# Padding between the pools of a hybrid attention and RWKV block, so that both operands of each 512-column product start at the same byte address modulo 512

## The chip, the core and the metric

The kernel runs on one core of one Trainium2 chip. The metric is the device time of one execution in microseconds (us). The engines are TensorE (PE; its weight loads are shown apart, as PEld), VectorE (DVE), ScalarE (ACT), GpSimd (POOL) and SyncE (SP, which only issues transfers here). They run independently, each with its own queue of instructions in program order, and meet at semaphores.

## The reference

One layer on x of 2048 rows and 1024 columns, in float32:

```python
h   = rms_norm(x, pre_mix_g);  proj = h @ w_in          # 1024 -> 5376 columns
y_a = chunk_band_attention(q, k, v, rel_bias)           # 8 heads, chunks of 64, 8 chunks back
y_b = rwkv7_time_mix(p_rwkv, ...)                       # 8 heads, a recurrence over time
merged = gate_a * (y_a @ proj_a) + gate_b * (y_b @ proj_b)
x = x + rms_norm(merged @ w_out, post_mix_g)
u = square(relu(rms_norm(x, pre_ffn_g) @ w_up)) @ w_down  # 1024 -> 4096 -> 1024
x = x + rms_norm(u, post_ffn_g)
```

## The kernel before

**Products in three terms.** Large products are not done in plain float32. Each operand is split into a rounded high part and a rest, both of the type float32r, and `mm3` (L73) adds three products: high times high, high times rest, rest times high. Each is one matmul with a stationary operand of 128x128 and a moving operand of 128x512, into one bank of PSUM. The split takes one cast on ACT (L70) and one subtraction on DVE (L71).

**Stages.** The 2048 rows are four groups of 512. For each group come: the RWKV part (`phase_rwkv`: dense products `psd` of `dense`, L89, then chunked linear algebra in plain float32, an inverse on DVE and the recurrence), the attention (`phase_attention`; it also computes the second branch product, `ps_p` of `branch`, with the RWKV output), and the merge (`phase_merge`: the first branch product, `ps_p`, then the output projection `ps_o`, L1028; the next group's norm runs beside it, in groups 0 to 2). After the four groups the feed-forward part runs in two halves, each an up stage (`phase_up`, `ps_u`) and a down stage (`phase_down`, `ps_dn`, L1290), both with one level of Strassen's scheme: seven products in place of eight.

**Where operands lie.** On-chip memory (SBUF) is given out in pools. A pool takes a stretch of each partition beside the pool that was opened before it, and gives each of its tiles a place there; pools that are marked "right" are stacked from the other end. A pool that closes leaves its place to the next. So the size of one tile shifts the start of all that lies behind it. Nothing in the kernel before chooses these starts; they follow from the sizes.

From the allocation of the two programs, the start of the moving and of the stationary operand of each 512-column float32r product, modulo 512 bytes:

| product | count | moving, stationary before | after |
|---|---|---|---|
| dense `psd` | 4032 | 320, 320 | 480, 480 |
| second branch `ps_p` (attention) | 384 | 320, 320 | 480, 480 |
| first branch `ps_p` (merge) | 384 | 480, 320 | 480, 480 |
| output projection `ps_o`, groups 0 to 2 | 576 | 320, 192 | 480, 480 |
| output projection `ps_o`, group 3 | 192 | 320, 320 | 480, 480 |
| up `ps_u` | 2688 | 320, 480 | 480, 480 |
| down `ps_dn` | 2688 | half 320, 320, half 480, 480 | 480, 480 |
| low-rank `ps_z`, `ps_a` (L327, L328) | 64 | 288, 320 | 320, 320 |
| gate `ps_g` (L661) | 48 | 288, 288 | 320, 320 |
| attention scores `ps_s` of 512 columns | 16 | 320, 320 | 480, 480 |

**What sets the order.** A scheduling layer (Tile) places each engine's instructions and adds the waits; a tile's place is free again when its last reader is done. So a tile that moves to other addresses can change what its first writer waits for. n2 (L391) is a small tile of the RWKV part: POOL fills it with ones (L392) and copies the reciprocal squared norms into it (L396), POOL and DVE read it (L399, L462, L487). n2t (L387) is what it is copied from. T (L506) is the workspace of the inverse, X (L505, L507) the inverse itself, which starts as a copy of the identity. The carry copies (L298, L299) hand the last column of one group to the next.

Of the kernel before, what the change touches and what calls it, by code (L numbers as in the profile page):

```python
# [9 lines left out]
F32 = mybir.dt.float32  # L10
# [8 lines left out]
P = 128  # L19
# [6 lines left out]
GT = G // P  # L26
C = 64
NC = G // C
# [14 lines left out]
def advance(steps, n=None):  # L43

    while n is None or n > 0:
        if next(steps, steps) is steps:
            return
        n = n and n - 1


class Block:
# [70 lines left out]
    def constants(self, ctx, mixing):  # L122
        tc, nc, a = self.tc, self.nc, self.a
        keep = ctx.enter_context(tc.tile_pool(name="const", bufs=1))
# [5 lines left out]
        nc.vector.memset(self.nhalf, -0.5)  # L130
        self.ssq = keep.tile([P, self.NG, GT, 2], F32, name="ssqo")
        self.g2c = keep.tile([P, KB], F32, name="g2c")
        self.bones = cp.tile([P, P], F32, name="bones")
        nc.vector.memset(self.bones, 0.0)
        for h in range(2):
# [208 lines left out]
    def rwkv_pre(self, g, p, rp, NA, between=lambda: None):  # L344
# [39 lines left out]
        pss = self.pa.tile([P, GT, 2], F32, tag="a", name="ps_ss")  # L384
        for t in range(GT):
            nc.tensor.matmul(pss[:, t], sq[:, t * P : (t + 1) * P], self.bones2, start=True, stop=True)
        n2t = self.tp.tile([P, GT, 2], F32, tag="n2t", bufs=2, name="n2t")  # L387
        nc.vector.tensor_scalar(n2t, pss, 1e-24, None, ALU.max)
        nc.vector.reciprocal(n2t, n2t)

        n2 = rp.tile([P, NC, 2], F32, tag="n2", name="n2")  # L391
        nc.gpsimd.memset(n2, 1.0)  # L392
        n2v = n2.rearrange("p (t h) e -> p h t e", h=2)
        for par in range(2):
# [103 lines left out]
    def rwkv_inverse(self, NA, rp):  # L498

        nc, ip = self.nc, self.ip  # L500
        N = ip.tile([P, 32, 32], F32, tag="N", name="N")
        nc.vector.transpose(
            N, NA.rearrange("p q c t -> p t (q c)")[:, 0:32, None, :].to_broadcast((P, 32, 2, 2 * NC))
        )
        X = ip.tile([P, 32, 16], F32, tag="X", name="X")  # L505
        T = ip.tile([P, 144], F32, tag="T", name="T")  # L506
        nc.scalar.copy(X, self.x0)  # L507
        for s in range(31):
            n, m = 31 - s, s // 2 + 1
            t = T[:, 0 : n * m].rearrange("p (a b) -> p a b", b=m)  # L510
            nc.vector.tensor_tensor(
                t,
                N[:, s + 1 : 32, s, None].to_broadcast((P, n, m)),
                X[:, s : s + 1, 0:m].to_broadcast((P, n, m)),
                ALU.mult,
            )
            nc.vector.tensor_tensor(X[:, s + 1 : 32, 0:m], X[:, s + 1 : 32, 0:m], t, ALU.add)
            yield
        X1 = ip.tile([P, 2, NC, 32], F32, tag="X1", name="X1")
        nc.vector.transpose(X1.rearrange("p q c (j d) -> p j d (q c)", d=2), X.rearrange("p r j -> p j r"))  # L520
        XD = ip.tile([P, 2, NC, 32], F32, tag="N", name="XD")
        nc.vector.transpose(XD, X1)
        XT = rp.tile([P, 2, NC, C], F32, tag="XT", bufs=1, name="XT")
        for par in range(2):
            r0 = par * C
            nc.gpsimd.memset(XT[r0 + 32 : r0 + 64, :, :, 0:32], 0.0)
            nc.scalar.copy(XT[r0 + 32 : r0 + 64, :, :, 32:64], XD[r0 + 32 : r0 + 64])
        for par in range(2):
            nc.scalar.copy(XT[par * C : par * C + 32, :, :, 0:32], XD[par * C : par * C + 32])
        self.X1, self.XT = X1, XT  # L530
# [406 lines left out]
    def phase_attention(self, g):  # L937
        tc, nc = self.tc, self.nc
        self.yctx = ExitStack()
        yp = self.yctx.enter_context(tc.tile_pool(name="ya", bufs=1, side="right", reuse_waits="tile"))  # L940
        self.ya = self.alloc_y(yp)
        self.bp = self.yctx.enter_context(tc.tile_pool(name="br", bufs=2, side="right", reuse_waits="tile"))
        with ExitStack() as ctx:
            e = ctx.enter_context
            self.ap = e(tc.tile_pool(name="at", bufs=2, reuse_waits="tile"))
            pp = e(tc.tile_pool(name="atp", bufs=1, reuse_waits="tile"))
            self.psc = e(tc.tile_pool(name="atps", bufs=1, space=PSUM, reuse_waits="tile"))
            self.pt = e(tc.tile_pool(name="atpt", bufs=1, space=PSUM, reuse_waits="tile"))
            self.pv = e(tc.tile_pool(name="atpv", bufs=2, space=PSUM, reuse_waits="tile"))
            self.pts, self.npt = [], 0  # L950
            for i in range(2):
                t = [pp.tile([P, 6, 2 * P], F32R, name=f"PT{x}{i}") for x in "hl"]
                for y in t:
                    nc.gpsimd.memset(y[:, 0, P : 2 * P].bitcast(F32), 0.0)
                    nc.gpsimd.memset(y[:, 5, 0:P].bitcast(F32), 0.0)
                self.pts.append(t)

            self.place = pp.tile([2 * GT, GT, P], F32, name="place")
            nc.gpsimd.memset(self.place, 1.0)
            pl = self.place.rearrange("e q (h d) -> e q h d", d=C)  # L960
            nc.gpsimd.affine_select(
                pl, pl, [[-1, GT], [-GT, 2], [0, C]], ALU.is_equal, 0.0, base=0, channel_multiplier=1
            )
            self.unscaled = {}
            beside = iter(())
            if g:
                beside = self.residual(
                    g - 1, pp, lambda: self.pd.tile([P, 4, P], F32, tag="d", name="ps_ht")
                )
            for p in range(NP):  # L970
                self.att_pair(g, p, beside)
            y = self.load_y()
            self.finish(NP - 1)
            for i in range(KB):
                nc.gpsimd.dma_start(self.md[i], self.branch(y, 1, i))
# [147 lines left out]
    def phase_up(self, half, zp, rp, cb, pn, early):  # L1123
# [6 lines left out]
        with ExitStack() as ctx:  # L1130
# [7 lines left out]
            X = zp.tile([P, 7, G], F32, tag="z", name="X")  # L1138
            T = {
                n: [tb.tile([P, KH, G], F32R, name=n + x) for x in "hl"] for n in ("t4", "b22", "t2", "t3", "t1")  # L1140
            }

            def operands():
                td, g1 = self.td[half], self.ht[2 * half + 1]
                for n, src in (
                    ("t2", td[:, 3]), ("t3", td[:, 1]), ("t1", td[:, 0]), ("b22", g1[:, hi4]), ("t4", td[:, 2])
                ):
                    h, l = T[n]
                    for k in (0, 2):
# [5 lines left out]
            def product(l, r, pool, tag):  # L1155
                ps = pool.tile([P, G], F32, tag=tag, name="ps_u")
                self.mm3(ps, [(l[0][:, k], l[1][:, k], r[0][:, k], r[1][:, k]) for k in range(KH)])
                return ps
# [11 lines left out]
            def hidden(dst, src, x):  # L1170

                nc.vector.tensor_tensor(dst, src, x, ALU.add)  # L1172
                nc.scalar.activation(dst, dst, AF.Relu)
                nc.scalar.activation(dst, dst, AF.Square)  # L1174
# [10 lines left out]
            def sums(i, x):  # L1185
                for o, l, r, op in ((3, X[:, 2], X[:, 1], ALU.add), (4, X[:, 3], x, ALU.subtract),
                                    (5, x, X[:, 2], ALU.subtract), (6, X[:, 0], X[:, 4], ALU.subtract)):
                    nc.vector.tensor_tensor(X[:, o], l, r, op)  # L1188
                    keep(o, i, X[:, o])
# [10 lines left out]
            for i in range(FF // P // 2):  # L1200
# [25 lines left out]
                w = up.tile([P, G], F32, tag="w", name="w")  # L1226
                nc.vector.tensor_tensor(q, p1, product(S2, T["t2"], pn, "dn"), ALU.add)
                if last is not None:
                    sums(*last)
                nc.vector.tensor_tensor(w, q, product(S3, T["t3"], pn, "dn"), ALU.add)  # L1230
                ps = product(S1, T["t1"], pn, "dn")
                hidden(X[:, 1], w, ps)
# [128 lines left out]
    def run(self):  # L1361
        tc, e = self.tc, None
        with ExitStack() as ctx, ExitStack() as mixing:
# [11 lines left out]
            for g in range(self.NG):  # L1375
                self.phase_rwkv(g, sums)
                self.phase_attention(g)
                with ExitStack() as c:
                    cmb = c.enter_context(tc.tile_pool(name="p1", bufs=1, reuse_waits="tile"))
                    sp = c.enter_context(tc.tile_pool(name="p0", bufs=2, reuse_waits="tile"))  # L1380
                    pt = c.enter_context(tc.tile_pool(name="p0p", bufs=2, space=PSUM, reuse_waits="tile"))
                    op = c.enter_context(tc.tile_pool(name="mo", bufs=1, reuse_waits="tile"))
                    b = cmb.tile([P, 4, G], F32, tag="cmb", name="cmb")
                    o = [op.tile([P, D], F32, name=f"o{t}") for t in range(GT)]
                    beside = next(sums)([b[:, i] for i in range(4)])
                    advance(beside, 1)
                    self.phase_merge(g, o, op, self.phase_norm(g + 1, sp, pt) if g + 1 < self.NG else iter(()), beside)
                    for t in range(GT):
                        self.nc.gpsimd.dma_start(self.od[g][t], o[t])
# [4 lines left out]
            rp = e(tc.tile_pool(name="raw", bufs=4, side="right", reuse_waits="tile"))  # L1394
# [58 lines left out]
```

## Time and profile before

| what | value |
|---|---|
| median of 3 runs | 3409.09 us (3408.39 to 3412.6) |
| profiled execution | 3405.34 us, with a span of 3403.6 us |
| mean granted TensorE clock | 0.984 |
| PE, PEld busy | 96%, 77% |
| DVE, ACT, POOL busy | 66%, 46%, 17% |
| DMA | 592.57 MB, mean 174 GB/s |

The span is the time from the first to the last instruction of the profiled execution. A row of the timeline gives start, duration, engine, line, operation, output and inputs, and how many equal instructions follow each other. In a row of windows the number behind "x" counts the instructions that lie in the stretch or reach over its edges. A matmul's own duration overlaps the next one's; how fast products run is read from the distance between their starts.

### The profile page before, as it was taken

Reading aid. Unit: us, or ns where it says so; the run is one execution under the profiler, and the core shown is the slowest. Engines: PE = TensorE matmul, PEld = TensorE weight load, DVE = VectorE, ACT = ScalarE, POOL = GpSimd, SP = SyncE. Lnnn points to the kernel's source line nnn. Section 1 sums busy time; section 2 is a strip of 40 time slices with the busy share of each in tenths; the row PEclk is TensorE's granted clock in tenths of the full one; section 3 lists DMA queues with packets and bytes.
Section 4 is the critical chain, followed back from the end, with each engine's and each line's share of the span. In section 5 each row is a group of like instructions: output and inputs, shape, how many; then the busy total and the mean of one; then the engine's idle time right before and its main releaser. Section 6 shows DMA issues by size and latency. Waiting matters only on the chain. (4 is left out here: it accounts for less than half of the span.)

```text
span 3403.6 us, 50503 instructions
## 1 busy us (share of the span) xinstructions
PE 3260.4 (96%) x18993; PEld 2623.8 (77%) x18993; DVE 2232.1 (66%) x3703; ACT 1576.3 (46%) x2575; POOL 593.5 (17%) x1101
## 2 busy tenths in 40 slices
PE   7999999999999999999999999999999999999998
PEld 5777777777877777877777787778788877787887
DVE  5775666775675775665766765777655657774465
ACT  4434634444644434654344654544543444454343
POOL 2122012122111222111221110122211111210000
PEclk9999999999999999999999999999999999999999
DMA  5235374246464236555325547654777875446565
GB/s 148 88 114 186 109 229 127 66 152 225 156 225 131 84 112 213 192 178 170 99 76 190 197 127 236 228 182 152 248 262 240 284 229 186 164 152 223 191 209 181
DMA packets 448669, 592.57 MB, mean 174 GB/s; under 512 B 26324, under 2 KB 313248, under 8 KB 448424
## 3 DMA queue, kind: packets, MB, share of 16 engines
q1 hardware_dynamic: 390184, 408.94, 38.6%
q0 software_dynamic: 49024, 163.61, 13.1%
q10 hardware_dynamic: 9216, 16.78, 1.4%
q8 instruction: 149, 2.44, 0.3%
q14 instruction: 96, 0.79, 0.1%
HBM read 425.37 MB, written 167.01 MB: 174 GB/s over the span
## 5 line engine op out<-in xcount | busy, mean ns | idle before, releaser
L1290 PE MATMUL ps_dn<-fop 128*128 128x512 f32 x2688 | 620.0, 393 | 8.4 <-ACT fop L70 5.8
L1290 PEld LDWEIGHTS ps_dn<-fop 128*128 128x128 f32 x2688 | 507.4, 189 | 119.0 <-ACT fop L70 6.6
L79 PE MATMUL psd<-hh,whi 128*128 128x512 f32 x1344 | 543.7, 405 | 12.2 <-ACT whi L70 8.2
L79 PE MATMUL psd<-hl,whi 128*128 128x512 f32 x1344 | 541.0, 402 | 0.0
L79 PE MATMUL psd<-hh,wlo 128*128 128x512 f32 x1344 | 538.5, 401 | 1.3 <-DVE wlo L71 1.3
L70 ACT CAST whi<-wraw 128x1024 fp32r<-128x1024 f32 (+1 forms) x296 | 255.6, 864 | 587.8 <-PE psd L79 383.9
L71 DVE TENSOR_TENSOR wlo<-wraw,whi 128x1024 fp32r<-128x1024 f32 (+1 forms) x296 | 293.1, 991 | 225.4 <-ACT whi L70 208.4
L79 PEld LDWEIGHTS psd<-hh,whi 128*128 128x128 f32 x1344 | 257.0, 191 | 65.0 <-ACT whi L70 8.9
L79 PEld LDWEIGHTS psd<-hh,wlo 128*128 128x128 f32 x1344 | 256.5, 191 | 51.3 <-DVE wlo L71 2.7
L79 PEld LDWEIGHTS psd<-hl,whi 128*128 128x128 f32 x1344 | 256.9, 191 | 49.8 <-issue 0.2
L71 DVE TENSOR_TENSOR fop<-xraw,fop 128x1024 fp32r<-128x1024 f32 x112 | 137.0, 1224 | 185.0 <-ACT fop L70 184.2
L70 ACT CAST fop<-xraw 128x1024 fp32r<-128x1024 f32 x112 | 117.5, 1049 | 265.9 <-PE ps_dn L1290 213.9
L1177 POOL DMA_DIRECT2D xd<-X x192 | 104.1, 542 | 406.2 <-ACT X L1174 351.8
L71 DVE TENSOR_TENSOR fop<-wdraw,fop 128x1024 fp32r<-128x1024 f32 x112 | 136.6, 1219 | 20.6 <-ACT fop L70 20.3
L70 ACT CAST fop<-wdraw 128x1024 fp32r<-128x1024 f32 x112 | 117.4, 1048 | 32.0 <-DMA wdraw<-in_w_down_dram 25.7
L857 DVE CUSTOM_DVE_ANT_0 sc<-bias,ps_s 128x640 f32<-128x640 f32 (+4 forms) x128 | 93.8, 733 | 57.7 <-PE ps_pt L868 31.9
L79 PE MATMUL ps_p<-yh,whi 128*128 128x512 f32 x256 | 105.1, 412 | 16.5 <-ACT whi L70 14.0
L872 ACT CAST PTh<-ps_pt 128x640 fp32r<-128x640 f32 (+4 forms) x128 | 80.0, 625 | 79.2 <-PE ps_pt L868 78.4
L70 ACT CAST s12h<-s 128x1024 fp32r<-128x1024 f32 x32 | 33.6, 1052 | 174.2 <-PE ps_u L79 174.2
L873 DVE TENSOR_TENSOR PTl<-ps_pt,PTh 128x640 fp32r<-128x640 f32 (+4 forms) x128 | 94.3, 737 | 29.6 <-ACT PTh L872 29.2
L862 ACT ACTIVATE sc<-sc,mn 128x640 f32<-128x640 f32 (+4 forms) x128 | 97.6, 763 | 19.2 <-DVE mn L857 18.4
L79 PE MATMUL ps_p<-yh,wlo 128*128 128x512 f32 x256 | 105.6, 413 | 0.6 <-DVE wlo L71 0.5
(368 smaller groups left out, 6879.2 us busy)
## 6 DMA issues: line engine op xcount, KB each, us to landing
wraw<-in_w_in_dram SPq DMA_DIRECT2D x168, 512.0 KB
xraw<-xd SPq DMA_DIRECT2D x112, 512.0 KB
xd<-X POOLq DMA_DIRECT2D x192, 256.0 KB, 5.1
wraw<-in_w_up_dram SPq DMA_DIRECT2D x80, 512.0 KB
wdraw<-wd SPq DMA_DIRECT2D x64, 512.0 KB
wdraw<-in_w_down_dram SPq DMA_DIRECT2D x48, 512.0 KB
gd<-gate ACTq DMA_DIRECT2D x64, 256.0 KB
cmb<-in_w_down_dram POOLq DMA_DIRECT2D x64, 256.0 KB, 4.7
```

What stands on the lines that cost most here:

```text
L70: self.nc.scalar.copy(hi, src)
L71: self.nc.vector.tensor_tensor(lo, src, hi.bitcast(F32), ALU.subtract)
L79: mm = nc.tensor.matmul(ps, l, r, start=n == 0, stop=n == last).ins
L857: nc.vector.tensor_tensor_reduce(sc[:, 0:n], bias[:, s0:640], pss[:, c0 : c0 + n], 1.0, 3.0e38, ALU.add, ALU.min, mn,)
L862: nc.scalar.activation(sc[:, 0:n], sc[:, 0:n], AF.Exp, scale=-1.0, bias=mn, accum_out=sm[:, col : col + 1])
L872: nc.scalar.copy(hv, pst[:, 0:nk])
L873: nc.vector.tensor_tensor(lv, pst[:, 0:nk], hv.bitcast(F32), ALU.subtract)
L1177: nc.gpsimd.dma_start(self.xd[q][i // 2][:, i % 2], src)
L1290: nc.tensor.matmul(ps, o[:, l, k, sl], o[:, r, k], start=start and n == 0, stop=stop and n == end)
```

## The change

Three tiles are added that nothing reads or writes: 160 bytes in the pool of constants, 320 bytes in the attention's pool (after the four head pairs, ahead of the tiles that hold the RWKV output), and 128 bytes in the norm's pool beside the merge, in groups 0 to 2. Two tiles get smaller: T has 136 numbers in place of 144, n2t one buffer in place of two. n2 leaves the RWKV pool of three buffers and goes to the pool of temporaries with two.

```diff
         self.g2c = keep.tile([P, KB], F32, name="g2c")
+        keep.tile([P, 40], F32, name="pad")
...
-        n2t = self.tp.tile([P, GT, 2], F32, tag="n2t", bufs=2, name="n2t")
+        n2t = self.tp.tile([P, GT, 2], F32, tag="n2t", bufs=1, name="n2t")
...
-        n2 = rp.tile([P, NC, 2], F32, tag="n2", name="n2")
+        n2 = self.tp.tile([P, NC, 2], F32, tag="n2", bufs=2, name="n2")
...
-        T = ip.tile([P, 144], F32, tag="T", name="T")
+        T = ip.tile([P, 136], F32, tag="T", name="T")
...
                 self.att_pair(g, p, beside)
+            self.ap.tile([P, 80], F32, tag="pad", bufs=1, name="pad")
             y = self.load_y()
...
                     sp = c.enter_context(tc.tile_pool(name="p0", bufs=2, reuse_waits="tile"))
+                    if g + 1 < self.NG:
+                        sp.tile([P, 32], F32, tag="pad", bufs=1, name="pad")
```

The order of instructions on PE and on SP is the same in both programs. On POOL and ACT a few move. On POOL, around the end of the second pair of group 1 (n2_5772 and n2_5775 are that pair's n2), before:

```order
L396 COPY n2_5772<-n2t_5769 64x4 x4
L399 TENSOR_TENSOR mN_5778<-mI_86,n2_5772 128x512 x2
L436 DMA bvd1_466<-r_5629 128x512
L299 COPY carry_96<-pr_6013 128x1
L298 COPY pr_6121<-carry_96 128x1
```

and now:

```order
L397 COPY n2_5775<-n2t_5772 64x4 x4
L400 TENSOR_TENSOR mN_5781<-mI_87,n2_5775 128x512 x2
L437 DMA bvd1_467<-r_5632 128x512
L393 MEMSET n2_6807 128x16
L300 COPY carry_97<-pr_6016 128x1
L299 COPY pr_6124<-carry_97 128x1
```

The ones-fill for the fourth pair's n2 now stands here, ahead of the carry copies; before, it stood behind the first pair, where now the third pair's fill stands. The fills for the first two pairs stand a few rows earlier than before. On ACT, at the start of group 1, before:

```order
L1036 ACTIVATE sqo,ssqo<-ps_o 128x512 x4
L70 CAST whi<-wraw 128x1024 x2
L297 COPY pr<-psd 128x512
L300 ACTIVATE lw<-psd,omu 128x512
L314 ACTIVATE lw<-lw 64x512
```

and now:

```order
L1038 ACTIVATE sqo,ssqo<-ps_o 128x512 x4
L70 CAST whi<-wraw 128x1024
L508 CAST X<-x_107 128x512
L70 CAST whi<-wraw 128x1024
L298 COPY pr<-psd 128x512
L301 ACTIVATE lw<-psd,omu 128x512
L315 ACTIVATE lw<-lw 64x512
```

The identity copy into X, which stood among the casts of the attention's end, now stands between the weight casts of the group's first two dense products. The same holds in groups 2 and 3.

## The prediction

> **What bounds the kernel now.** I read the page's busy times first, then the waits of TensorE, then how closely its products follow each other, stage by stage.
>
> ```profile
> span 3403.6 us, 50503 instructions
> PE 3260.4 (96%) x18993; PEld 2623.8 (77%) x18993; DVE 2232.1 (66%) x3703; ACT 1576.3 (46%) x2575; POOL 593.5 (17%) x1101
> ```
>
> TensorE (PE) is busy for 96% of the span, and the rest is scattered. A busy PE is not a PE at its peak, though, so the question is the pace: the time from the start of one 512-column product to the start of the next. Two stages of the feed-forward part show it without disturbance. The first row is one unbroken run of 879 down products; the others are a window of the up stage, one of the down stage, and the first product of two neighbouring up sums (twelve products apart).
>
> ```profile
> 3149.83 200.34 PE L1290 MATMUL ps_dn<-fop 128*128 128x512 f32 x879
> ...
> 3000.00:3050.00 50.00, 50.00 (x216) 1.00 0.44 140
> ...
> 3150.00:3200.00 50.00, 50.00 (x221) 1.00 0.60 194
> ...
> 3001.02 0.39 PE L79 MATMUL ps_u<-t4h,s3h 128*128 128x512 f32 x1
> ...
> 3003.82 0.39 PE L79 MATMUL ps_u<-bh,a1h 128*128 128x512 f32 x1
> ```
>
> Down: (200.34 - 0.39)/878 = 227.7 ns. Up: (3003.82 - 3001.02)/12 = 233.3 ns, and the windows agree (a window counts products that reach over an edge, so 50.39/216 = 233.3 and 50.39/221 = 228.0). Granted clock 1.00 and PE busy for all 50 us in both: no wait makes the difference of 5.6 ns.
>
> From the allocation of the two programs I compared the start addresses of both operands, modulo 512 bytes. Of 11,072 products of 512 columns in float32r, 3,712 have unequal starts before: 2,688 in the two up stages (moving 320, stationary 480), 576 in the output projection of groups 0 to 2 (320 and 192), 384 in the merge's branch product (480 and 320) and 64 of the low-rank products (288 and 320). All down products and all dense ones are equal. (The weights that load during a product are the next one's; inside a sum they start at the same remainder as its own.) After the change none of the 11,072 is unequal.
>
> Is it the offset, or the stage? The output projection is the natural experiment: the same line, shape and loop, unequal in groups 0 to 2, equal in group 3. Below are first and last rows of an unbroken run in group 0 (23 rows), the same in group 3 (28 rows), then a run of dense products (26 rows, both operands at 320) and one of the merge's branch products (17 rows, unequal).
>
> ```profile
> 519.09 0.39 PE L1028 MATMUL ps_o<-wlo,mh 128*128 128x512 f32 x1
> ...
> 524.20 0.40 PE L1028 MATMUL ps_o<-whi,ml 128*128 128x512 f32 x1
> ...
> 2109.66 0.39 PE L1028 MATMUL ps_o<-whi,ml 128*128 128x512 f32 x1
> ...
> 2115.78 0.40 PE L1028 MATMUL ps_o<-whi,ml 128*128 128x512 f32 x1
> ...
> 530.17 0.39 PE L79 MATMUL psd<-hh,whi 128*128 128x512 f32 x1
> ...
> 535.83 0.39 PE L79 MATMUL psd<-hl,whi 128*128 128x512 f32 x1
> ...
> 996.07 0.40 PE L79 MATMUL ps_p<-yh,whi 128*128 128x512 f32 x1
> ...
> 999.82 0.40 PE L79 MATMUL ps_p<-yl,whi 128*128 128x512 f32 x1
> ```
>
> Unequal group 0: 5.11/22 = 232.3 ns. Equal group 3: 6.12/27 = 226.7. Dense, equal: 5.66/25 = 226.4. Merge, unequal: 3.75/16 = 234.4. So in every stage that I looked at, equal starts go with 226 to 228 ns and unequal ones with 232 to 234, and equal at 320 is as good as equal at 480 (the down stage has both).
>
> One rule speaks against this. The Trainium skill, "TensorE: Matmul & The Clock Gate", § Part 2, says of TensorE's two read ports that loading the next weights takes no read bandwidth from the running product; "SBUF — State Buffer", § Who interferes with whom, says: "PE and ACT never wait on anyone." By these, no start address could matter and the change would be worth 0. The rows of group 0 against group 3 disagree, and no row explains those 5.6 ns otherwise; I keep the rule as a rival.
>
> **The change part by part.** No product, transfer or arithmetic changes, and the order on PE and SP is the same row by row. What moves is where operands start.
>
> *Up stages.* 2,688 products x (233.3 - 227.7) = 15.1 us. Is PE what sets the end there? The first rows are the two up stages and the second down stage (busy time of PE, its weight loads, DVE, ACT and POOL, then granted clock and DMA share), then come PE's waits in the first up stage, all of them.
>
> ```profile
> 2116.00:2433.60 317.60, 314.78 (x1346) 252.13 (x1345) 230.04 (x314) 157.03 (x221) 60.01 (x112) 1.00 0.58 194
> ...
> 2757.40:3082.40 325.00, 318.97 (x1345) 255.10 (x1346) 232.42 (x318) 155.50 (x219) 60.36 (x112) 0.98 0.56 186
> 3082.20:3392.50 310.30, 308.21 (x1345) 252.94 (x1343) 165.73 (x166) 123.62 (x144) 12.46 (x23) 0.99 0.61 201
> ...
> PE ps_u L79 <- ACT s3h L70: 1.4, 1, 1.4
> PE ps_u L79 <- ACT s12h L70: 0.9, 1, 0.9
> PE ps_u L79 <- DVE s3l L71: 0.5, 1, 0.5
> ```
>
> PE waits 2.8 us in 317.6; VectorE (DVE) is busy 72%, ScalarE (ACT) 49%, the transfers 58%. A stage shorter by 7.5 us leaves DVE at 74%. I count all of it.
>
> *Output projection.* 576 x (232.3 - 227.7) = 2.6 us; its runs are gapless, so all of it.
>
> *Merge's branch product.* 384 x (234.4 - 227.7) = 2.6 us of PE time, but this stage waits for its weights:
>
> ```profile
> 979.00:1011.40 32.40, 26.39 (x107) 19.89 (x106) 21.10 (x33) 11.93 (x21) 5.11 (x10) 0.95 0.92 306
> ...
> L70 ACT CAST whi<-wraw 128x512 fp32r<-128x512 f32 x8 | 5.0, 620 | 14.1 <-DMA wraw<-in_proj_a_dram 11.2 <-PE ps_p L79 2.2 <-DMA wraw<-in_w_out_dram 0.7
> ```
>
> Transfers take 92% of it, and the cast of the weights sat idle 11.2 us for DMA: a faster PE waits longer for the next weights. I take 0; the ends are 0 and 2.6.
>
> *Low-rank products.* 64 x 5.6 = 0.4 us at most, between other work: I take 0.
>
> *What the pools move.* The ones-fill of n2 (L392) is now in a pool of two buffers, so on POOL it comes after each of the first two pairs of a group and not only after the first; there it waits for DVE's last read of the older n2. Behind it stand the carry copies (L299, L298), which every later mix needs.
>
> ```profile
> DVE NA L487: 39.3, 4
> ...
> 81.37 0.11 POOL L392 MEMSET n<- 128x16 f32 x1 [9.71 <-DVE NA L487]
> 85.06 0.76 POOL L299 COPY carry<-pr 128x1 f32<-128x1 f32 x1 [3.58 <-ACT pr L297]
> ...
> 108.41 0.59 POOL L436 DMA_DIRECT2D bvd<-r  x1 [2.76 <-DVE r L435]
> 123.71 0.18 POOL L299 COPY carry<-pr 128x1 f32<-128x1 f32 x1 [14.71 <-ACT pr L297]
> ...
> 117.55 0.41 DVE L494 TENSOR_TENSOR BR<-ps_A,mN 128x256 f32<-128x256 f32 x1
> ```
>
> After pair 0 the wait is old (four of them, 39.3 us of POOL idle before L392; in group 0 9.71 us, and the carry copy still waited 3.58 us for ACT afterwards). After pair 1 the new one ends with L494 at 117.96, and the next POOL row starts at 123.71: 5.7 us of slack, so 0. If the slack were gone it would cost as much as the fill is late. The identity copy X on ACT moves out of the attention into the start of the next group:
>
> ```profile
> 434.41 0.62 ACT L507 CAST X<-x 128x512 f32<-128x512 bf16 x1
> 528.94 1.04 ACT L70 CAST whi<-wraw 128x1024 fp32r<-128x1024 f32 x1
> 533.54 1.05 ACT L70 CAST whi<-wraw 128x1024 fp32r<-128x1024 f32 x1 [3.56 <-PE psd L79]
> ```
>
> There it falls into 3.56 us in which ACT waits for PE: 0; without that cover 3 x 0.62 = 1.9 us. The one buffer less of n2t and the shorter T shorten no product of the inverse (its largest has 136 numbers) and cost 0.
>
> *Sum.* 15.1 + 2.6 = 17.7 us. The profiled execution took 3405.34 us for a span of 3403.6; it becomes 3387.6 with a span of 3385.9. The median of the runs, 3409.09, is 3.75 us above the profiled execution, so I forecast **3391.4 us**. Its own range is 3384 to 3396: at the low end every unequal product reaches the best pace seen (226.4) and none is hidden, 2,688 x 6.9 + 576 x 5.9 + 384 x 8.0 + 0.4 = 25.4 us; at the high end only the up stages gain and the copy of X costs its 1.9 us, 3409.1 - 15.1 + 1.9 = 3396.
>
> **The rivals.** (A) *The start does not matter*: the up stage is slow because of its neighbours (DVE 230 us of 317.6 there, 166 of 310.3 in the second down stage, and more ACT), and the group 0 runs because transposes stand between them. Then the time stays at 3409. For it: within the up stage nothing is equal, so there is no comparison inside it. Against it: three unequal stages with very different neighbours share 232 to 234 ns. This is also what the two pages' rule would give.
>
> (B) *The up stage is handed to its feeders*: the casts and subtractions of the weights (L70, L71) are late once PE is quicker, and half of the 15.1 us returns as waits. For it: those are the three waits that exist. Against it: 2.8 us in 317.6. Time 3409.1 - 7.5 - 2.6 = 3399.
>
> (C) *Slower: the fill of n2 holds POOL.* Behind pair 1 in each group the fill waits as long as it does behind pair 0, and the mix behind it stops PE. By the row of L392 that wait is 9.71 us; four groups make 38.8, and it decides once it exceeds the 5.7 us of slack by more than 17.7/4 = 4.4 us a group. At 9.71 beyond the slack: 3409.1 - 17.7 + 38.8 = 3430. Against it: L494 of pair 1 ends before the carry copy can start in any case.
>
> **How the numbers follow.** Forecast 0.80, A 0.10, B 0.07, C 0.03. A difference of under 0.2% (6.8 us) cannot be told from none here. Forecast and B are both faster by more: 0.87; A is the same: 0.10; C slower: 0.03. The range 3384 to 3401 holds the forecast's own range and B, and leaves out A and C and a little beyond, below 2 in 10.
>
> **What would show it.** Right: 50 us windows inside the up stages count 221 products, not 216; the first up stage lasts about 310 us, not 317.6; the second down stage stays near 310.3, since its operands were equal already; the output projection of group 0 runs at 227 ns. A: the up window still counts 216. B: 221 there, but waits of PE for L70 or L71 of over 7 us. C: POOL idle before L392 doubles from four to eight times and PE waits behind L301. Were the up stage to reach 227.7 and the total not to fall, the sum's claim that PE sets the end there would be wrong.

## The result, and the profile after

| | before | after |
|---|---|---|
| median, timed side by side | 3408.74 us (3406.22 to 3412.6) | 3393.28 us (3387.05 to 3396.91) |
| ratio to before | | 0.9951, interval 0.9936 to 0.9967 |
| profiled execution, its span | 3405.34, 3403.6 us | 3390.85, 3389.1 us |

The change is faster by half a per cent: 16.7 us (11 to 22) of 3409 by the ratio, 15.5 us between the two medians. The forecast was 3391.4 us. Of all executions behind this document one, of the kernel "up only" below, took 8084.17 us and enters no ratio. The page after, its first rows:

```profile
span 3389.1 us, 50514 instructions
PE 3241.7 (96%) x18993; PEld 2625.3 (77%) x18993; DVE 2230.9 (66%) x3703; ACT 1575.4 (46%) x2575; POOL 591.9 (17%) x1101
```

Nothing is busier or idler by share. PE's busy time falls by 18.7 us, though it runs the same 18,993 products: on average each takes less. The windows that answer to those of before are the two up stages, the second down stage, and 50 us inside an up and a down stage (busy time of PE, its weight loads, DVE, ACT and POOL, then granted clock and DMA share):

```profile
2119.70:2430.40 310.70, 307.43 (x1345) 253.13 (x1344) 229.14 (x314) 156.87 (x221) 59.92 (x112) 0.99 0.59 197
2751.30:3068.60 317.30, 310.63 (x1344) 254.99 (x1345) 230.94 (x317) 155.49 (x219) 60.20 (x112) 0.98 0.57 191
...
3000.00:3050.00 50.00, 50.00 (x222) 41.42 (x221) 35.43 (x50) 24.85 (x36) 8.63 (x16) 1.00 0.50 170
3150.00:3200.00 50.00, 50.00 (x222) 41.40 (x221) 25.09 (x24) 17.59 (x18) 0.00 (x0) 1.00 0.61 196
...
3068.60:3378.70 310.10, 307.05 (x1345) 253.04 (x1343) 166.40 (x167) 123.72 (x144) 12.44 (x23) 0.99 0.62 203
```

The up stages took 317.4 us (2116.0 to 2433.4) and 324.8 us (2757.4 to 3082.2); they take 310.7 and 317.3. The 50 us of the up stage held 216 products and hold 222, now as many as the down stage. The second down stage, counted over as many products as before, stays: 310.3 to 310.1 us.

The timeline after gives the pace: the first products of two up sums twelve apart, then the first and last of an unbroken run of the output projection in group 0 (23 rows), then a run of 937 down products.

```profile
3000.63 0.39 PE L79 MATMUL ps_u<-t3h,s3h 128*128 128x512 f32 x1
...
3003.35 0.39 PE L79 MATMUL ps_u<-t1h,s12h 128*128 128x512 f32 x1
...
515.83 0.40 PE L1030 MATMUL ps_o<-wlo,mh 128*128 128x512 f32 x1
...
520.82 0.39 PE L1030 MATMUL ps_o<-whi,ml 128*128 128x512 f32 x1
...
3139.83 212.55 PE L1292 MATMUL ps_dn<-fop 128*128 128x512 f32 x937
```

Up 2.72/12 = 226.7 ns, output projection 4.99/22 = 226.8, down 212.16/936 = 226.7. Over whole stages (mean distance between the starts of neighbouring products of one line, distances of 300 ns and more left out):

| product | before, ns | after, ns |
|---|---|---|
| up | 233.3 | 226.8 |
| output projection, groups 0 to 2 | 232.5 | 227.2 |
| first branch (merge) | 234.9 | 228.8 |
| down | 227.7 | 226.8 |
| dense | 228.2 | 228.5 |

The two rows that the forecast called equal before are the two that hardly move, the dense one not at all.

By stages the span changes so: up stages -6.7 and -7.5 us, down stages -3.1 and -0.9, everything ahead of them +3.7; together -14.5. The waits of PE in the first up stage are those of before with 0.5 us more, 3.3 in place of 2.8:

```profile
PE ps_u L79 <- ACT s3h L70: 1.5, 1, 1.5
PE ps_u L79 <- ACT s12h L70: 0.9, 1, 0.9
PE ps_u L79 <- DVE s3l L71: 0.5, 1, 0.5
PE ps_u L79 <- ACT z L1196: 0.4, 1, 0.4
```

On POOL the fill of n2 (now L393) waits eight times, and the timeline of group 0 shows the second of them with the carry copy behind it (L300):

```profile
POOL n L393 <- DVE NA L488: 73.4, 8, 9.9
...
117.87 0.11 POOL L393 MEMSET n<- 128x16 f32 x1 [8.30 <-DVE NA L488]
124.27 0.19 POOL L300 COPY carry<-pr 128x1 f32<-128x1 f32 x1 [6.29 <-ACT pr L298]
```

The fill waits 8.30 us, and the copy behind it then still waits 6.29 us for ACT: the wait that was added lies wholly inside one that was there.

### The profile page after: what moved, and what is told of

Same layout as the page of the kernel before. It is cut to its first block, busy times and chain, and to the rows that moved or that the text cites. A ratio compares the mean times of both kernels' runs of the same rounds, so it can differ in the third digit from the quotient of the medians.

```text
span 3389.1 us, 50514 instructions
## 1 busy us (share of the span) xinstructions
PE 3241.7 (96%) x18993; PEld 2625.3 (77%) x18993; DVE 2230.9 (66%) x3703; ACT 1575.4 (46%) x2575; POOL 591.9 (17%) x1101
## 5 line engine op out<-in xcount | busy, mean ns | idle before, releaser
L71 DVE TENSOR_TENSOR wlo<-wraw,whi 128x1024 fp32r<-128x1024 f32 (+1 forms) x296 | 293.4, 992 | 226.8 <-ACT whi L70 211.2
```

Of the source, the lines that this page charges most:

```text
L71: self.nc.vector.tensor_tensor(lo, src, hi.bitcast(F32), ALU.subtract)
```

## The experiments

The theory: a 512-column product is slower by some 6 ns when its moving operand and the weights start at different addresses modulo 512, and PE sets the end in the up stages. The rival: something else in the change, or in the up stage, carries the gain.

**One part alone, and all but that part.** A small unused tile ahead of the feed-forward part's pools makes the up products' starts equal in the kernel before (40 numbers, "up only"), and unequal again in the changed one (88 in their place, "mix only").

```diff
  mixing.close()
  e = ctx.enter_context
+ e(tc.tile_pool(name="ffpad", bufs=1, reuse_waits="tile")).tile([P, 40], F32, name="pad")
  zp = e(tc.tile_pool(name="z", bufs=2, reuse_waits="tile"))
```

Up only:

> The kernel before with one dead tile of 160 bytes opened after the four groups, ahead of the feed-forward pools: only the up stages' operands (2,688 products) and the half of the down tiles that began at 320 move to 480; everything up to the feed-forward part is the kernel before. Theory (the start of the operands sets the pace of the up stages): the up stages run at about 227 ns a product and the time falls by 15 us, to 3392 to 3396. Rival (the gain of the change comes from the moved fills, copies or waits of the mixing part): the time stays at 3406 to 3412 and the up windows still count 216 products in 50 us.

Mix only:

> The whole change, with one dead tile of 352 bytes opened ahead of the feed-forward pools, which brings the up stages back to unequal starts (320 and 480); the mixing part keeps the change. Theory with the prediction's sum: 2.6 us less than before for the output projection, 3404 to 3408. Rival, read from the trace of the change (the first up stage begins at 2119.7 us, 2116.0 before): what the projection gains is given back while the groups wait for weights or run at half clock, and the time is 3408 to 3413, no gain.

The changed kernel, beside them:

> The change itself once more, timed beside the others. Its first four executions lie between 3387 and 3397. Theory: 3388 to 3397 again, and equal to the run with only the up stages' starts changed within 4 us.

Measured, with a median of 3409.99 us for the kernel before: up only 3403.03 us, ratio 0.9978 (0.9969 to 0.9987); mix only 3419.35, ratio 1.0033 (1.0023 to 1.0043); the changed kernel 3388.62, ratio 0.9939 (0.9927 to 0.9952). The pace did what the theory says: up products at 226.8 ns in "up only", 233.4 in "mix only". The time did not. The waits of PE between 2105 and 2140 us, of SP between 2080 and 2131, and windows from the end of the last merge on show why, all in "up only":

```profile
PE ps_u L79 <- ACT bh L1111: 10.4, 1, 10.4
...
SPq L1119 <- DMA od<-o: 11.9, 1, 11.9
...
2119.70:2130.40 10.70, 0.26 (x3) 0.01 (x1) 1.74 (x4) 2.09 (x5) 2.50 (x6) 0.68 0.88 316
2130.40:2137.30 6.90, 6.44 (x15) 4.74 (x16) 4.88 (x4) 3.69 (x5) 0.00 (x0) 0.51 1.03 413
```

The tile moved everything behind it, and the place of bl, the first operand that the feed-forward part loads (L1119), came to wait for tiles of the last merge: its load stood 11.9 us on SP until an output (od) had been stored. PE stood still for 10.4 us, and the next 6.9 us ran at a granted clock of 0.51. "Mix only" has the same wait of 10.4 us. So both runs measured the offset and a price of their own pad together; by an estimate from the two windows, 10.4 us of standing still and half of 6.9 us, that price is 14 us. Neither time came out as it was expected. With the 14 us taken off, up only would be some 21 us under the kernel before and mix only some 3; as the price is an estimate, the two runs show nothing against the theory and do not size it.

**The same two, without the late load.** The unused tile now stands at the other end of memory, in a pool ahead of the up products' weights, which move from 480 to 320; in the kernel before that makes them equal to the moving operand (320), in the changed one unequal (480).

```diff
  up = e(tc.tile_pool(name="up", bufs=1, reuse_waits="tile"))
+ e(tc.tile_pool(name="opspad", bufs=1, side="right", reuse_waits="tile")).tile([P, 40], F32, name="pad")
  sp = e(tc.tile_pool(name="ops", bufs=1, side="right", reuse_waits="tile"))
```

Up stages equal, all else as before:

> The kernel before with 160 unused bytes beside the pool that holds the up products' weights, so that they start at 320 modulo 512 like the moving operand (2,688 products made equal, nothing else moved, the first loads of the feed-forward part untouched). Theory (the start offset sets the pace, PE sets the end): up products at 227 ns, each up stage about 7 us shorter, median 3409 - 15 = 3394 us (3391 to 3398). Rival (the other tiles of the change carry the gain): 3407 to 3410. The earlier run with the pad at the other end came to 3403, with PE held 10.4 us at the start of the up stage; if that wait was the pad's doing, it is not here.

Up stages unequal, all else as changed:

> The kernel after with the same 160 unused bytes, so that the up products' operands start at 480 (moving) and 320 (stationary) again, everything else as after. Theory: up products back at 233 ns, median about 3391 + 15 = 3406 us (3402 to 3409), so the rest of the change is worth 0 to 4 us (the down stages' pace and the output projection's, less what the merge gives back). Rival (the rest of the change carries the gain): under 3398.

Measured against 3409.13 us: the first 3395.38 us, ratio 0.9953 (0.9941 to 0.9965), which is -16 us (-20 to -12); the second 3408.3 us, ratio 0.9997 (0.9988 to 1.0005), -1 us (-4 to +2). The windows of the first up stage and of 50 us in the second, of the first kernel and then of the second:

```profile
2121.80:2432.60 310.80, 307.57 (x1346) 253.00 (x1345) 228.64 (x314) 156.59 (x221) 59.83 (x112) 0.99 0.59 198
...
3000.00:3050.00 50.00, 50.00 (x222) 41.42 (x221) 35.96 (x49) 24.61 (x34) 9.29 (x18) 1.00 0.56 188
```

```profile
2115.50:2433.80 318.30, 315.71 (x1346) 252.82 (x1345) 231.03 (x315) 157.05 (x222) 60.51 (x114) 1.00 0.58 194
...
3000.00:3050.00 50.00, 50.00 (x215) 40.17 (x214) 37.53 (x52) 25.58 (x36) 10.49 (x20) 1.00 0.50 162
```

In the first, no operation, transfer or place in the queues differs from the kernel before, the wait of 10.4 us is gone (PE has two waits of 0.8 us together around the stage's start), and the stage falls from 317.4 to 310.8 us; in the second it is back at 318.3. One unused tile of 160 bytes gives nearly all of the measured gain (16 us, where the whole change gave 16.7 in its first series and 21 in its second), and takes it away. The rest of the change, as timed, is worth -1 us, which cannot be told from nothing. It may hide a little: the second kernel's up products run at 234.3 ns and not at the 233.3 of before, and its two up stages last 0.9 and 1.1 us longer than before, so without that the rest would be worth about -3 us.

The first kernel also shows that 320 is as good a common start as 480. The second has its moving operand at 480, as the changed kernel has, and is slow: the start of one operand alone does not count. Its operands lie 160 bytes apart; before, they lay 352 apart, which modulo 512 is 160 the other way. Both directions cost about the same.

**Only the rests shifted.** Two operands meet in each product: its own weights, and the weights of the next one, which load beside it. In the changed kernel both start alike. To tell them apart, in the kernel before with "up only"'s pad the high parts and the rests of one operand were put at different starts: in the first up stage those of the weights (320 and 480, moving always 480), in the second those of the moving operand (480 and 128, weights always 480).

```diff
- T = {n: [tb.tile([P, KH, G], F32R, name=n + x) for x in "hl"] for n in ("t4", "b22", "t2", "t3", "t1")}
+ T = {n: [] for n in ("t4", "b22", "t2", "t3", "t1")}
+ for x in "hl":
+     for n in T:
+         T[n].append(tb.tile([P, KH, G], F32R, name=n + x))
+     if half == 1 and x == "h":
+         tb.tile([P, 40], F32, name="pad")
...
+ if half == 0:
+     for x in "hl":
+         for tag, n in (("a1", KB), ("s12", KB), ("s3", KB), ("s4", KH)):
+             sp.tile([P, n, P], F32R, tag=tag + x, name="place")
+         if x == "h":
+             sp.tile([P, 40], F32, tag="pad", name="pad")
```

> As the run with only the up stages moved, but in the first up stage the stationary high parts start at 320 and the rests at 480 (all moving parts at 480); in the second up stage only the moving rests start at 128, the rest at 480. Products come in threes: high x high, high x moving rest, stationary rest x high. If a product's own weights must start as its moving operand does, the first and second of each three in the first up stage are slow (233 ns and more) and the third fast (227). If it is the next product's weights, which load while this one streams, the first and third are slow and the second fast. In the second up stage both expect the second alone to be slow. If starts do not matter, all are alike.

Measured: 3410.42 us (3409.99 before), with the late load in it. In the first stage the three products of a triple ran alike, 229.6, 230.0 and 230.4 ns; in the second 234.3, 231.1 and 231.4. No single product carries the price, so neither theory holds as it was put (the trace of the down stages, below, gives a reason). What this arrangement cannot do is keep one pair equal and the other unequal throughout.

**Alternating starts.** This one can. It builds on the changed kernel; high parts of both operands lie at 320, rests at 480, and each sum of twelve products takes them in a fixed sequence: hh, ll for "own" (weights first, h for high, l for rest), hl, lh for "cross", ll, lh or ll, hl where one operand alternates, hl or lh alone for "all unequal". The lines that place the parts are left out here.

```diff
- self.mm3(ps, [(l[0][:, k], l[1][:, k], r[0][:, k], r[1][:, k]) for k in range(KH)])
+ n = next((n for n in T if r is T[n]), "b")
+ mode = MODES[half][n]
+ for j in range(12):
+     a, b = mode[j % len(mode)]
+     nc.tensor.matmul(ps, l["hl".index(a)][:, j % KH], r["hl".index(b)][:, j % KH], start=j == 0, stop=j == 11)
```

> Which pair has to start alike? The up products take rounded parts from two places, so that a stationary operand starts at 320 or 480 and a moving one at 320 or 480, in five fixed sequences of twelve products: own (320 with 320, then 480 with 480: each product equal to its own weights, unequal to the next), cross (stationary 320 with moving 480, then 480 with 320: unequal to its own weights, equal to the next), two sequences in which only the moving or only the stationary start alternates, and two in which all twelve are unequal; the bh products (all 480) are the control. The sums leave out terms (two of the three kinds of product at most), so only the pace counts. If a product must match its own weights: own 227 ns, cross 234. If it must match the weights that load beside it (the next): own 234, cross 227. Either of the two: 230 to 231 where one alternates. If it is the change of place from product to product: own and cross both over 230, with the steady unequal sequences at 233 to 234 as before.

Mean pace in ns, in the first and the second up stage:

| sequence | first | second |
|---|---|---|
| all 480 (control) | 227.3 | 227.6 |
| own: equal to its own weights, unequal to the next | 234.4 | 234.2 |
| cross: unequal to its own, equal to the next | 229.3 | 229.6 |
| weights stay at 480, moving alternates | 231.4 | 230.6 |
| moving stays at 480, weights alternate | 229.9 | 230.0 |
| all unequal (weights 320, moving 480; and the reverse) | 234.7 | 233.3 |

The timeline of the second stage shows it sum by sum: 24 control products, then one sum each of cross (t2), own (t3) and all unequal (t1).

```profile
3000.14 5.64 PE L1180 MATMUL ps_u<-bl,a1l 128*128 128x512 f32 x24
3005.62 0.39 PE L1180 MATMUL ps_u<-t2l,s12h 128*128 128x512 f32 x1
...
3008.39 0.40 PE L1180 MATMUL ps_u<-t3h,s3h 128*128 128x512 f32 x1
...
3011.20 2.96 PE L1180 MATMUL ps_u<-t1h,s12l 128*128 128x512 f32 x12
3013.99 0.39 PE L1180 MATMUL ps_u<-b22l,s4l 128*128 128x512 f32 x1
```

5.48/24 = 228.3, then 2.77/12 = 230.8, 2.81/12 = 234.2 and 2.79/12 = 232.5. A product that matches its own weights alone gains nothing: 234.3 ns is the pace of the unequal ones. One that matches the weights loading beside it alone gains part of the price in the mean. But it does not come to 227 as was expected: from the fifth product of a sum on, cross runs at 230.0 ns, in steps (distances from one start to the next) of 224 and 236, and the two sequences in which one operand alternates run at 229.7 to 230.2 as well. So which meeting makes the price is not settled; being equal to the next weights is no better here than being equal to everything half of the time.

The trace of the kernel before shows why single steps cannot be read as prices of single products. In the down stages 48 products lie at 320, the next 48 at 480, and so on. Each product is equal to its own weights, and only the last of each 48 meets weights that start elsewhere, the next product's: a seam. Below are eleven products from such a last one on, and eleven from the tenth after it:

```profile
3162.57 2.71 PE L1290 MATMUL ps_dn<-fop 128*128 128x512 f32 x11
...
3164.89 2.66 PE L1290 MATMUL ps_dn<-fop 128*128 128x512 f32 x11
```

(2.71 - 0.39)/10 = 232 ns, then (2.66 - 0.39)/10 = 227 ns. In the mean over both down stages, the ten steps from such a seam on take 237, 229, 233, 236, 224, 231, 236, 228, 233 and 231 ns where 320 goes over to 480, and 228, 236, 233, 236, 224, 231, 236, 228, 233 and 231 the other way; then 226.7. One seam costs 49 to 50 ns, spread over ten products, of which nine are equal to their own weights and to the next. (At a seam both operands also change their place; whether the unequal meeting or the change does it is not shown.) A sequence that repeats every two or three products never gets clear of what went before. How two reads of different starts come to disturb each other stays open.

**Ten distances.** On "up only", each group of up products got its own distance between the starts.

```diff
- T = {n: [tb.tile([P, KH, G], F32R, name=n + x) for x in "hl"] for n in ("t4", "b22", "t2", "t3", "t1")}
+ T, at = {}, 0
+ for n, d in zip(("t4", "b22", "t2", "t3", "t1"), ((32, 64, 96, 128, 160), (192, 256, 320, 416, 448))[half]):
+     if d > at:
+         tb.tile([P, (d - at) // 4], F32, name="pad" + n)
+     at = d
+     T[n] = [tb.tile([P, KH, G], F32R, name=n + x) for x in "hl"]
```

> Up products with the moving operand shifted against the stationary one by 32, 64, 96, 128 and 160 bytes (first up stage: t4, b22, t2, t3, t1) and by 192, 256, 320, 416 and 448 (second), the bh products equal as a control. Known: 0 bytes 226.7 ns, 352 bytes 233.3. If the penalty is a clash of two fixed streams it shows at some offsets only (some at 227, some at 233 or more); if anything unequal costs the same, all ten are at 232 to 234; if it goes by the distance, it rises from 32 to 256 and falls again to 448. bh at 227 in each case. Time: 3395 to 3412, with the same late start of the up stage as in the earlier run with a pad at that end.

Measured 3410.51 us, with the late load, and by distance:

| bytes | 0 | 32 | 64 | 96 | 128 | 160 | 192 | 256 | 320 | 416 | 448 |
|---|---|---|---|---|---|---|---|---|---|---|---|
| ns | 227.4 | 233.4 | 231.3 | 233.8 | 233.0 | 234.3 | 233.3 | 230.1 | 230.1 | 233.6 | 232.6 |

The rows are the first products of the sums t3 (416), t1 (448), b22 (256), t4 (192) and then 24 bh products (0) in the second stage:

```profile
3001.22 0.39 PE L79 MATMUL ps_u<-t3h,s3h 128*128 128x512 f32 x1
...
3004.03 0.39 PE L79 MATMUL ps_u<-t1h,s12h 128*128 128x512 f32 x1
...
3006.82 0.39 PE L79 MATMUL ps_u<-b22h,s4h 128*128 128x512 f32 x1
...
3009.58 0.39 PE L79 MATMUL ps_u<-t4h,s3h 128*128 128x512 f32 x1
...
3012.38 0.39 PE L79 MATMUL ps_u<-bh,a1h 128*128 128x512 f32 x1
...
3017.84 0.40 PE L79 MATMUL ps_u<-t2h,s12h 128*128 128x512 f32 x1
```

234.2, 232.5, 230.0, 233.3 and 227.5 ns. Nine of the ten distances cost, 32 bytes as much as 352, and it does not rise with the distance. The mean at 256 misleads: its sums follow those at 448, and their steps are, in the mean of 16 sums, 228, 230, 233, 236, 225, 231, 235, 228, 232, 231, 227 and 227 ns, which is what equal starts show behind a seam; the last two are at the pace of equal ones. So 256 bytes probably cost nothing, though two products of each sum are too few to show it. The control's 227.4 has the same tail in it: its last six steps take 226.7. At 320 the last six of a sum still take 228.9, at 64 they take 231.4. The ten distances and the control lie side by side within the two up stages, five in each, so a different load of DVE or ACT hardly explains them.

## Why the prediction was right, point by point

*The pace.* "Equal starts go with 226 to 228 ns and unequal ones with 232 to 234" holds in the stages after the change within a nanosecond (226.8 to 228.8) and in the experiments that turn it on and off with one unused tile. As a rule for any distance it is too simple: unequal starts gave 229 to 235 ns, and 256 bytes perhaps nothing.

*Up stages, 15.1 us.* Measured 14.2 in the two traces, and 16 (12 to 20) by the times of the kernel that changes only that. The product gained more than forecast, 233.3 - 226.8 = 6.5 ns and not 5.6, since the 227.7 that stood for "equal" was taken from down products that themselves changed start between tiles. 2,688 x 6.5 = 17.5 us, and 14.2 of it shows in the stages. In the first, 8.7 us became 6.7: PE waited 0.5 us more, and the stage's granted clock fell from 1.00 to 0.99. In the second, 8.7 became 7.5, and why is open. That 15.1 lies so near to the measured times is in part luck: a pace step taken too small, and a share taken as whole.

*Output projection, 2.6 us.* The pace came as forecast (226.8 against 226.7), but "its runs are gapless, so all of it" is the step that did not hold up. The part ahead of the feed-forward stages did not get shorter. It ends at 2116.2 us in the trace before and at 2119.9 after; over all traces it ends between 2116.2 and 2122.0 with the old layout there (five, mean 2120.0) and between 2115.7 and 2122.7 with the new one (five, mean 2119.3). The kernel with everything but the up stages came to -1 us (-4 to +2), or about -3 with its slower up products taken off. What the traces show beside it are longer waits for the weights of these stages. Before, then after: ACT's casts waiting for the transfers of the projections, and PE in the output projection waiting for the casts.

```profile
ACT whi L70 <- DMA wraw<-in_proj_a_dram: 47.6, 23, 5.4
ACT whi L70 <- DMA wraw<-in_w_out_dram: 36.3, 21, 4.2
...
PE ps_o L1028 <- ACT whi L70: 1.3, 4, 0.5
```

```profile
ACT whi L70 <- DMA wraw<-in_proj_a_dram: 52.6, 24, 6.4
ACT whi L70 <- DMA wraw<-in_w_out_dram: 41.0, 23, 4.2
...
PE ps_o L1030 <- ACT whi L70: 5.4, 8, 1.6
```

9.7 us more idle for transfers on ACT, 4.1 us more on PE. That fits a stage that its transfers hold, as the forecast had said of the merge next door; but the kernel with the old layout there and equal up stages waited 2.6 us at the same place, so part of it is the spread of the runs. That the 2.6 us went there is likely and not shown.

*Merge's branch product, taken at 0.* Its pace gained 6.1 ns, and no gain can be seen: as forecast.

*What was left out: the down stages.* They were counted as equal already, and took 4.0 us less in the traces. The forecast's remark that the next weights "start at the same remainder" inside a sum does not hold here: a sum runs over tiles at 320 and at 480, and every 48 products there is a seam, with its 49 to 50 ns. After the change there are no seams; 2,688 x (227.7 - 226.8) = 2.4 us of the 4.0, and the rest is open. Its effect on the time, like the output projection's, is inside the -1 us of the kernel without the up stages.

So the mechanism was right, and the total came out near the forecast because the up term is nearly all of it; the 2.6 us of the output projection and the missed gain of the down stages are within what the runs cannot tell apart.

*The rivals.* A, the start does not matter: refuted, the windows count 222 and not 216, and one tile moves 16 us. The Trainium skill, "SBUF — State Buffer", § Who interferes with whom, says that "PE and ACT never wait on anyone"; within PE, between equal and unequal starts of its two reads, the runs disagree, with 6.5 ns in 233. B, the feeders take half back: PE waits 3.3 us in the first up stage against 2.8. C, the fill holds POOL: it did wait eight times, 73.4 us against 39.3, but the row at 124.27 shows 6.29 us of slack left in group 0, where 5.7 were reckoned, so there it never came to the point from which it decides; in the other three groups the copy behind the fill still waited 5.39 us for ACT.

## What to carry to other kernels

When two stages run the same product at different paces with PE busy throughout and the granted clock at 1.00, compare the start addresses of the moving operand and of the weights, its own and the next ones, modulo 512: one unused tile of 160 bytes was worth half a per cent of this kernel. Give all of a stage's operands one common start, tiles at seams included, and do not stop at "close": 32 bytes apart cost as much as 352. Then look at what the pad moves: the same 160 bytes at the wrong end made the first load of the next stage wait for old tiles, and 3403 us came out in place of 3395: half of the gain was gone.

## What the runs showed of the hardware that was not expected

- Starting like its own weights does nothing for a product whose next weights start elsewhere: 234.3 ns, where both equal give 226.7 and all unequal 233.3 to 234.7.
- One seam, at which operands with one common start follow on others, slows about ten products, together by 49 to 50 ns, though nine of them have equal starts.
- A distance of 32 bytes costs 6 ns of 227, as much as 352; at 320 some 2 ns remain, and at 256 probably none.
- A gap on PE costs more than itself: after 10.4 us of standing still the next 6.9 us ran at a granted clock of 0.51, where the kernel before, without the gap, had 1.00.
